# Seven products for the query weights and for the later convolution's second group, paired splits, and query norms moved into the sigmoids

## The chip, the cores and the metric

The kernel runs on one core of one Trainium2 chip. The core has a matrix engine (TensorE, PE in the profile, with its weight loads as PEld), a vector engine (VectorE, DVE), a scalar engine (ScalarE, ACT), GpSimd (POOL) and a sync engine (SyncE, SP). DMAs are issued from the queues of SP, ACT and POOL. The metric is the time of one execution on the device in microseconds (us); lower is better.

## What is computed

Two layers, each on the same 512 tokens of width 2048. A layer normalises its input, multiplies it by one wide input matrix, feeds three mixers, joins them and multiplies by an output matrix; the result is added to the input. In short:

```python
h = rmsnorm(x, norm_g); proj = h @ w_in            # 512 x 2048 @ 2048 x 7696
y_conv = B * (conv3(C * H) + bias) * silu(G)        # 512 channels, width 3, causal
q = rmsnorm(sb_q, qn_g); k = rmsnorm(sb_k, kn_g)    # 8 heads of 128, norm over a head
z = (q * 128**-0.5) @ k.T                           # strictly causal
later = reversed_cumsum(log_sigmoid(-z)) - log_sigmoid(-z)
y_sb = (exp(log_sigmoid(z) + later) @ v) * silu(g)
y_gla = rmsnorm(gated_linear_attention(...)) * silu(gl_g)
x = x + concat(y_conv, y_sb, y_gla) @ w_out         # 2048 x 2048
```

Inputs and outputs are float32. The kernel works in pairs of float16 parts (a high part and what is left), so that each product of two such operands is three matmuls: high by high, high by low, low by high.

## The kernel before

**Weights.** The input matrix and the output matrix are taken in groups of 256 columns. Each layer has, in this order: six groups of the linear attention; four of the first convolution half (h, c, g, b); for each of four pairs of heads (j = 0 to 3) values, gate, queries and keys (v, g, q, k); four of the second convolution half, which the code calls `conv h 1`, `conv c 1`, `conv g 1` and `conv b 1`; and eight groups of the output projection. `fetch` (line 346) loads a group of 2 MB into one of two staging buffers, two groups ahead, from POOL's queue. While PE works on one group, the next is prepared: `wmax` sums squares on ACT (L366), `wscale` sums over partitions on POOL (L380) and forms a power of two, and the parts are made: the high part on ACT and the low part on DVE. The squares are tied behind the first matmul of the running group and the preparation behind a later one (`hook`, line 466).

**Plain groups** (`project_cols`, `project_toks`, `project_by_token`) use the parts as they are: 96 matmuls of 512 moving columns, or 192 of 256, for 2048 rows. `whi` and `wlo` make the parts in two halves of 128x2048 (L435 on ACT, L442 on DVE).

**Seven-product groups** (`project_quick`, line 749) cut input, weights and result into two by two quarters and form the result from seven quarter products in place of eight (the scheme of Strassen and Winograd). The sums of the inputs are made once a layer (`xsums`, `msums`); they live in a buffer that the loaded mix of the branches takes later. The sums of the weights are made for each group in `wsums` (line 471): one addition by an accumulating DMA issued on POOL (L503) for the input matrix, the others on DVE (L506, L508, L511), and seven splits of 128x1024 (L485 on ACT, L486 on DVE). The names in `QUICK_IN` (line 31) and `QUICK` say which groups go this way: before, the gates and the keys of all pairs, `conv h 1`, and three and four groups of the output projection. The seven products go into four accumulators, pa and pd in one PSUM bank of 512 columns, pb and pf in another; between them ACT and DVE copy and add the intermediate results into the output tile (L778 to L792).

**Attention.** The queries and keys of a pair are projected (line 1298 on). For each, ACT squares every head of every token with a sum (L1318), DVE forms a reciprocal square root with three Newton steps on 8 columns (`rsqrt_bits`), and multiplies it into the tile: once for the queries (L1327), in eight products with the gains for the keys (L1332). Then high and low parts are made and SP transposes them by DMA (L1341). `attend` queues four later steps, which run after the following groups through `go`: `scores` for each of two heads, then `values` for each. `scores` takes the four query tiles of a head in two chunks of two tiles (`CHUNKS`): the products with the keys (L1226), the causal mask, two sigmoids (L1234, L1236), running products along the keys (L1239), a product, parts, and their transposes (L1247). `values` multiplies with v (L1263), then with the gate (L1270).

**The mix.** Each branch's result is scaled and split (`mixsplit`) and, until `mixload` (line 881), written to DRAM. `mixload` issues six loads on SP, after the group `conv h 1`. After the gate of the second convolution half, `weight_ratio` finds one common scale (L178) and rescales what was loaded, and the output projection follows.

**Order.** Outside of the first stretch, a planner in the compiler's front end puts each engine's instructions in order by its own estimate of their times; the order in the text gives the priority, and the preparation of weights is raised above it. On the chip every engine goes through its own queue in that fixed order, and waits at semaphores.

## Time and profile before

| what | value |
| --- | --- |
| median of 3 runs | 1718.91 us (1718.07 to 1722.91) |
| the profiled execution | 1717.69 us |
| its span, first to last instruction | 1715.9 us |
| mean granted clock of PE | 0.992 |
| DMA packets, bytes | 181478, 227.26 MB |
| chain: PE, DVE, DMA, ACT, issue | 73%, 12%, 7%, 4%, 3% |

A row of a group reads: line, engine, operation, output<-inputs, shapes, count, then busy us, the mean ns of one, and the engine's idle time before them with what ended it. A row of a window reads: the window in us from the span's start, its length, the busy time of PE, PEld, DVE, ACT and POOL with counts, the granted share of PE's clock, the mean busy share of the 16 DMA engines, and GB/s. A row of the timeline reads: start, length, engine, line, operation; in square brackets the engine's idle time before it and what ended it. Matmuls are pipelined, so a row's length is longer than the distance between the starts of two.

### The profile page before, as it was taken

Reading aid. Unit: us, or ns where it says so; the run is one execution under the profiler, and the core shown is the slowest. Engines: PE = TensorE matmul, PEld = TensorE weight load, DVE = VectorE, ACT = ScalarE, POOL = GpSimd, SP = SyncE. Lnnn points to the kernel's source line nnn. Section 1 sums busy time; section 2 is a strip of 40 time slices with the busy share of each in tenths; the row PEclk is TensorE's granted clock in tenths of the full one; section 3 lists DMA queues with packets and bytes.
Section 4 is the critical chain, followed back from the end, with each engine's and each line's share of the span. In section 5 each row is a group of like instructions: output and inputs, shape, how many; then the busy total and the mean of one; then the engine's idle time right before and its main releaser. Section 6 shows DMA issues by size and latency. Waiting matters only on the chain.

```text
span 1715.9 us, 36876 instructions
## 1 busy us (share of the span) xinstructions
PE 1669.9 (97%) x15642; PEld 1298.4 (76%) x15642; DVE 1331.3 (78%) x2327; ACT 1129.1 (66%) x1619; POOL 239.2 (14%) x286
## 2 busy tenths in 40 slices
PE   7999999999999989999989999999999999899999
PEld 5644548989898964799976455689898889548998
DVE  8975889877878767785688677997786888677883
ACT  7667677767666656666665676776765767565662
POOL 1211111111111111001122101121111111101110
PEclk9999999999999999999999999999999999999999
DMA  7233323566766686245543332446666667753441
GB/s 251 83 114 98 99 64 99 145 116 152 136 149 139 147 233 164 77 150 181 186 103 108 116 102 75 118 123 125 148 136 105 146 132 150 201 153 108 162 151 50
DMA packets 181478, 227.26 MB, mean 132 GB/s; under 512 B 94194, under 2 KB 141628, under 8 KB 180800
## 3 DMA queue, kind: packets, MB, share of 16 engines
q0 software_dynamic: 60352, 168.83, 34.4%
q1 hardware_dynamic: 111952, 46.61, 14.4%
q10 hardware_dynamic: 9008, 9.45, 1.7%
q8 instruction: 122, 2.00, 0.5%
q14 instruction: 44, 0.36, 0.1%
HBM read 179.65 MB, written 14.68 MB: 113 GB/s over the span
## 4 chain that ended last, share of the span: by engine, by line
PE 73%; DVE 12%; DMA 7%; ACT 4%; issue 3%; POOL 0%; DVEq 0%; ACTq 0%
PE psp L767 13%; PE psp L674 8%; PE psp L675 8%; PE psp L673 8%; PE psp L685 7%; PE psp L684 7%; PE psp L683 7%; PE psp L814 6%; PE psp L764 3%; DMA st<-in_w_in_dram 2%; DVE wl L486 2%; DMA th<-za 2%; DMA kT<-qp 2%; ACT junk L366 1%; DVE wl L442 1%
## 5 line engine op out<-in xcount | busy, mean ns | idle before, releaser
L366 ACT ACTIVATE junk<-st 128x2048 uint8<-128x2048 f32 x150 | 285.1, 1901 | 44.1 <-DMA st<-in_w_in_dram 42.8
L442 DVE SCALAR_TENSOR_TENSOR wl<-st,ws,wh 128x2048 f16<-128x2048 f32 x102 | 239.2, 2347 | 80.7 <-ACT wh L435 80.7
L435 ACT ACTIVATE wh<-st,ws 128x2048 f16<-128x2048 f32 x100 | 199.3, 1998 | 105.4 <-PE psp L674 47.1
L684 PE MATMUL psp<-wl,m 128*128 128x256 f16 x960 | 261.7, 273 | 0.0
L683 PE MATMUL psp<-wh,m 128*128 128x256 f16 x960 | 261.7, 273 | 0.0
L685 PE MATMUL psp<-wh,m 128*128 128x256 f16 x960 | 261.7, 273 | 0.0
L485 ACT ACTIVATE wh<-st,ws 128x1024 f16<-128x1024 f32 x150 | 167.6, 1143 | 120.5 <-DVE st L506 57.7
L486 DVE SCALAR_TENSOR_TENSOR wl<-st,ws,wh 128x1024 f16<-128x1024 f32 x150 | 189.6, 1279 | 27.4 <-ACT wh L485 27.3
L355 POOL DMA_DIRECT2D st<-in_w_in_dram x114 | 102.2, 900 | 436.0 <-DVE wl L442 319.4
L683 PE MATMUL psp<-wh,x 128*128 128x256 f16 x512 | 139.6, 273 | 0.0
L684 PE MATMUL psp<-wl,x 128*128 128x256 f16 x512 | 139.6, 273 | 0.0
L685 PE MATMUL psp<-wh,x 128*128 128x256 f16 x512 | 139.6, 273 | 0.0
L675 PE MATMUL psp<-x,wl 128*128 128x512 f16 x352 | 134.4, 382 | 2.2 <-DVE zun L186 2.2
L674 PE MATMUL psp<-x,wh 128*128 128x512 f16 x352 | 134.4, 382 | 0.0
L673 PE MATMUL psp<-x,wh 128*128 128x512 f16 x352 | 134.0, 381 | 0.0
L673 PE MATMUL psp<-m,wh 128*128 128x512 f16 x352 | 133.9, 380 | 0.0
L674 PE MATMUL psp<-m,wh 128*128 128x512 f16 x352 | 133.9, 380 | 0.0
L675 PE MATMUL psp<-m,wl 128*128 128x512 f16 x352 | 133.9, 380 | 0.0
L675 PEld LDWEIGHTS <-wl 128*128 128x128 f16 x704 | 69.2, 98 | 85.0 <-DVE wl L442 2.7
L673 PEld LDWEIGHTS <-wh 128*128 128x128 f16 x704 | 69.2, 98 | 81.5 <-issue 3.1
L380 POOL PARTITION_ALL_REDUCE wgm<-wm x75 | 40.0, 533 | 648.2 <-ACT junk L366 633.6
L674 PEld LDWEIGHTS <-wh 128*128 128x128 f16 x704 | 69.2, 98 | 80.8 <-issue 2.3
(427 smaller groups left out, 4042.2 us busy)
## 6 DMA issues: line engine op xcount, KB each, us to landing
st<-in_w_in_dram POOLq DMA_DIRECT2D x114, 1024.0 KB, 8.4
st<-in_w_out_dram POOLq DMA_DIRECT2D x32, 1024.0 KB, 7.4
st<-st POOLq DMA_DIRECT2D x18, 512.0 KB, 8.3
st<-in_w_in_dram SPq DMA_DIRECT2D x6, 1024.0 KB, 12.0
mixd<-g POOLq DMA_DIRECT2D x24, 256.0 KB, 7.7
x<-in_x_dram SPq DMA_DIRECT2D x4, 1024.0 KB, 4.9
qT<-in_x_dram ACTq DMA_DIRECT2D x8, 512.0 KB, 3.8
qT<-xs ACTq DMA_DIRECT2D x8, 512.0 KB, 3.9
```

What stands on the lines that cost most here:

```text
L366: sq = S.activation(junk(HK * GW).rearrange("p (k n) -> p k n", k=HK), staged[i][h], AF.Square, accum_out=peak[i][:, h:h + 1])
L435: hi = S.activation(wh[:, :, :GW], staged[i][h], AF.Copy, scale=scales[i])
L442: V.scalar_tensor_tensor(wl[:, :, :GW], staged[i][h], scales[i], wh[:, :, :GW], ALU.mult, ALU.subtract)
L485: hi = S.activation(h_, b, AF.Copy, scale=sc)
L486: V.scalar_tensor_tensor(l_, b, sc, h_, ALU.mult, ALU.subtract)
L673: T.matmul(o, wh[:, kk, cs], xh[:, :, k, :], start=st_, stop=False)
L674: T.matmul(o, wh[:, kk, cs], xl[:, :, k, :], start=False, stop=False)
L675: mm = T.matmul(o, wl[:, kk, cs], xh[:, :, k, :], start=False, stop=en)
L683: T.matmul(o, ah[:, t, k, :], wh[:, kk, :n], start=st_, stop=False, skip_group_check=True)
L684: T.matmul(o, ah[:, t, k, :], wl[:, kk, :n], start=False, stop=False, skip_group_check=True)
L685: return T.matmul(o, al[:, t, k, :], wh[:, kk, :n], start=False, stop=en, skip_group_check=True)
L767: mm = T.matmul(o[:, t * P:(t + 1) * P], a[p_][:, t, kk, :], w[q_][:, kk, :], start=st_, stop=en, skip_group_check=True)
```

## The change

- The queries of all four pairs and `conv c 1` become seven-product groups, in both layers: ten groups more.
- `fetch` lays such a group out with the quarters side by side, so that two quarters are adjacent; it takes three DMAs instead of two. `wsums` splits two quarters at once: three splits of 128x2048 and one of 128x1024 instead of seven of 128x1024. In the output projection the order of the additions is that of the input projection.
- The product into pf goes ahead of the first one into pb, and the preparation of the next group is tied behind it.
- The queries are no longer divided by their norms: the gains go onto the queries, the norms of the queries become the scale of the sigmoids, one column for each query tile and head, so each sigmoid is split by query tile. One reciprocal square root on 16 columns serves queries and keys, after the keys.
- The second chunk of a head takes its query tiles in falling order, so that `values` ends in one operation instead of two.
- `mixload` is called after `conv c 1` instead of after `conv h 1`.

```diff
-QUICK_IN = ("g 0", "k 0", "g 1", "k 1", "g 2", "k 2", "g 3", "k 3", "conv h 1")
+QUICK_IN = ("conv h 1", "conv c 1") + tuple(f"{n} {j}" for n in "gqk" for j in range(4))
-CHUNKS = ((((3, 0), (2, 512)), (3, 2)), (((0, 0), (1, 128)), (0, 1)))
+CHUNKS = ((((3, 0), (2, 512)), (3, 2)), (((1, 0), (0, 256)), (1, 0)))
...
+        if i in quick:
+            w = src[l, :, c0:c0 + GW].rearrange("(k r p) n -> p r k n", p=P, r=2)
+            own = whole[i].rearrange("p (k r) c -> p k (r c)", r=2)
+            for o, r, c in ((0, 1, slice(P, GW)), (P, 0, slice(0, GW)), (P + GW, 1, slice(0, P))):
+                queue.dma_start(own[:, :, o:o + c.stop - c.start], w[:, r, :, c])
+            st.extend(own[:, :, h * GW:(h + 1) * GW] for h in range(2))
+            return
...
-        G.dma_start(out=b12, in_=b11, accum_op=ALU.add)
-        split(b11, 0)
-        split(b22, 3)
+        if specs[i][1] is w_out:
+            V.tensor_tensor(b12, b12, b11, ALU.add)
+        else:
+            G.dma_start(out=b12, in_=b11, accum_op=ALU.add)
+        split(own[:, :, :2 * P])
         V.tensor_tensor(b22, b12, b22, ALU.add)
-        split(b22, 1)
         V.tensor_tensor(b11, b22, b11, ALU.subtract)
-        split(b11, 2)
-        split(b21, 4)
+        split(own[:, :, :2 * P])
+        split(own[:, :, 2 * P:])
         V.tensor_tensor(b21, b22, b21, ALU.add)
-        split(b12, 5)
-        split(b21, 6)
+        split(b21)
...
             prod(pa, w11, a11, True)
             S.activation(y12, za, AF.Copy)
-            hook(prod(pb, wT2, s_, True))
+            hook(prod(pf, w22, a12_s, True))
+            prod(pb, wT2, s_, False)
             V.tensor_tensor(y21, zb, y12, ALU.subtract)
             prod(pd, wT3, a11_21, False)
             S.activation(y22, zd, AF.Copy)
-            prod(pf, w22, a12_s, False)
             prod(pa, w21, a12, False)
             S.activation(y11, za, AF.Copy)
             prod(pb, wt1, a21_22, False, True)
...
-            if j:
-                mixload()
             then()
             uc = wk([P, 2, seq], "raw", 1) if j else wk([P, 2, seq], "zw")
             ps, u = project(True, lambda: uc)
...
+            if j:
+                mixload()
...
-                    S.activation(a, z[:, :zw], AF.Sigmoid, scale=nzun[:, l:l + 1])
                     w = wk([P, zw], "zw")
-                    S.activation(w, z[:, :zw], AF.Sigmoid, scale=zun[:, l:l + 1])
+                    for m, dst in ((0, a), (8, w)):
+                        for t, o in qtiles:
+                            ts_ = slice(o, o + (t + 1) * P)
+                            S.activation(dst[:, ts_], z[:, ts_], AF.Sigmoid,
+                                         scale=qz[:, m + 2 * t + hh:m + 2 * t + hh + 1])
...
-                rs = sm(8, "qr")
-                rsqrt_bits(rs, sq, u2, 8, "q")
-                V.tensor_scalar(rs, rs, u, None, ALU.mult)
-                if gain is None:
-                    r8 = raw.rearrange("p a (h c) -> p (a h) c", c=P)
-                    V.tensor_tensor(r8, r8, rs.rearrange("p (a o) -> p a o", o=1).to_broadcast([P, 8, P]), ALU.mult)
+                V.tensor_scalar(rm[:, 8 * n:8 * n + 8], sq[:, 8 * n:8 * n + 8], u2, EPS, ALU.mult, ALU.add)
+                r8 = raw.rearrange("p a (h c) -> p (a h) c", c=P)
+                if not n:
+                    qu = sm(1, "qu")
+                    V.tensor_scalar(qu, u, nzun[:, l:l + 1], 2.0 ** 25, ALU.mult, ALU.mult)
+                    by = kg[:, l, :].rearrange("p (o c) -> p o c", o=1)
                 else:
-                    for t in range(NT):
-                        for hh in range(2):
-                            rp = raw[:, t, hh * P:(hh + 1) * P]
-                            V.scalar_tensor_tensor(rp, rp, rs[:, 2 * t + hh:2 * t + hh + 1], gain, ALU.mult, ALU.mult)
...
+                    rs = rsqrt_bits(rm, "q")
+                    qz = sm(16, "qz")
+                    V.tensor_scalar(qz[:, :8], rs[:, :8], qu, None, ALU.mult)
+                    V.tensor_scalar(qz[:, 8:], qz[:, :8], -1.0, None, ALU.mult)
+                    V.tensor_scalar(rs[:, 8:], rs[:, 8:], u, None, ALU.mult)
+                    by = rs[:, 8:].rearrange("p (a o) -> p a o", o=1)
+                V.tensor_tensor(r8, r8, by.to_broadcast([P, 8, P]), ALU.mult)
```

More of the change, by code (lines that the diff above doesn't have):

```diff
@@ L473, in wsums @@
         sc = scales[i]
[L474 removed]
+        own = whole[i].rearrange("p (k r) c -> p k (r c)", r=2)
+        b22, b11, b12, b21 = (own[:, :, n * P:(n + 1) * P] for n in range(4))
         parts = loaded[i][0]
[L476 to L478 removed]
@@ L503, in wsums, with split @@
-        G.dma_start(out=b12, in_=b11, accum_op=ALU.add)
-        split(b11, 0)
-        split(b22, 3)
+        def split(src):
+            n = src.shape[2] // P
+            if n == 1:
+                pair = [wk([P, HK * P], t, 1, dt=F16) for t in ("w7h", "w7l")]
+            else:
+                pair = [wpool.tile([P, HK, GX], F16, tag=t, name=nm(t)).rearrange("p k c -> p (k c)")[:, :HK * n * P]
+                        for t in ("wh", "wl")]
+            h_, l_ = (a.rearrange("p (k c) -> p k c", c=n * P) for a in pair)
+            S.activation(h_, src, AF.Copy, scale=sc)
+            V.scalar_tensor_tensor(l_, src, sc, h_, ALU.mult, ALU.subtract)
+            parts.extend([a[:, :, m * P:(m + 1) * P] for a in (h_, l_)] for m in range(n))
@@ L1297, in hybrid_trunk @@
             qkT = []
-            for gain in (None, kg[:, l, :]):
+            sq, rm = sm(16, "qs"), sm(16, "qrm")
+            for n in range(2):
                 raw = []
                 def dst():
-                    raw.append(wk([P, NT, GW], *(("raw", 1) if gain is None else ("kT",))))
+                    raw.append(wk([P, NT, GW], *(("kT",) if n else ("raw", 1))))
                     return raw[0]
@@ L1343, in hybrid_trunk @@
                 go()
-            attend(j, *qkT, vh, vl, vu, g, s_)
+            attend(j, *qkT, qz, vh, vl, vu, g, s_)
         conv_out(1, conv_in(1, go), go)
```

56 lines of the change are left out of this document (15 added, 41 removed).

## The prediction

> **What bounds the kernel now.** I read the busy table and the chain of waits first, to see which engine sets the end; then single weight groups, to price one group on TensorE (PE); then PE's waits; then the vector engine (DVE) and the scalar engine (ACT) over one pair of heads, to see what room they have.
>
> ```profile
> span 1715.9 us, 36876 instructions
> PE 1669.9 (97%) x15642; PEld 1298.4 (76%) x15642; DVE 1331.3 (78%) x2327; ACT 1129.1 (66%) x1619; POOL 239.2 (14%) x286
> PE 73%; DVE 12%; DMA 7%; ACT 4%; issue 3%; POOL 0%; DVEq 0%; ACTq 0%
> ```
>
> PE is busy 97% of the span and holds 73% of the chain: work taken off PE counts, as long as the others keep up. Windows cut at the first matmul of a group and of the next one:
>
> ```profile
> core 0: us, PE busy (x) PEld busy (x) DVE busy (x) ACT busy (x) POOL busy (x), PEclk, DMA share, GB/s
> 327.56:346.32 18.76, 18.76 (x338) 18.75 (x336) 15.94 (x31) 15.91 (x31) 4.33 (x5) 1.00 0.50 133
> 346.32:367.28 20.96, 20.96 (x195) 18.80 (x193) 14.11 (x33) 10.98 (x18) 2.00 (x2) 1.00 0.92 159
> 657.38:678.10 20.72, 20.72 (x99) 9.41 (x97) 15.86 (x25) 11.16 (x14) 2.30 (x3) 1.00 0.55 114
> 433.00:519.00 86.00, 85.73 (x951) 77.87 (x949) 69.20 (x125) 59.71 (x94) 14.29 (x17) 1.00 0.67 145
> ```
>
> The first row is the keys of pair 0, a group by seven products (336 matmuls, the count takes in neighbours at the edges; PE never idle): 18.76 us. The second is a plain group by tokens, values of pair 1 (192 matmuls): 20.96 us, 0.1092 us each. The third is a plain group by columns, gate of the later convolution (96 matmuls, 20.72 us). The last is one whole pair of heads (keys to keys): PE 85.73 of 86.00, DVE 69.20, ACT 59.71.
>
> **The PE term.** Eight query groups go from 20.96 to 18.76: 8 x 2.20 = 17.6 us. The later convolution's second group becomes 7 x 24 = 168 matmuls of 256 columns instead of 96 of 512: 168 x 0.1092 = 18.3 against 20.7, so 2 x 2.4 = 4.8 us. Together **-22.4 us**. Everything else must be hidden beside PE, or it comes off this.
>
> **The load of the mix halves, moved behind one more group.**
>
> ```profile
> PE psz L1226 <- DMA kT<-qp: 11.0, 2, 5.9
> 530.73 3.93 SPq L1341 DMA_TRANSPOSE kT<-qp  x2
> 617.17 7.09 SPq L887 DMA_DIRECT2D m<-mixd  x4
> 625.02 13.34 SPq L1341 DMA_TRANSPOSE kT<-qp  x2
> 640.15 0.69 PE L1226 MATMUL psz<-kT,qT 128*128 128x512 f16 x2 [5.87 <-DMA kT<-qp]
> 634.00:641.00 7.00, 1.13 (x5) 0.36 (x3) 0.63 (x1) 0.00 (x0) 0.00 (x0) 0.82 1.22 190
> 641.00:656.00 15.00, 15.00 (x65) 6.60 (x64) 8.94 (x12) 7.01 (x7) 1.78 (x2) 0.86 0.61 206
> 1493.00:1507.00 14.00, 14.00 (x65) 6.39 (x64) 8.34 (x11) 6.42 (x7) 1.79 (x2) 0.92 0.65 216
> ```
>
> PE's two longest waits inside the layers (11.0 us, one per layer) are the last pair's first scores waiting for the key transposes. In pair 2 SP handles the two key transposes in 3.93 us; in pair 3 four loads of the mix stand ahead, the DMA share is 1.22, and they take 13.34. After each wait the granted clock is low: 0.86 over 15 us and 0.92 over 14 us, so 0.14 x 15 + 0.08 x 14 = 3.2 us more. The six loads now come after the second convolution group (they must: that group reads the input sums whose buffer they overwrite), so nothing stands ahead of these transposes. With 4 us instead of 13 they land some 9 us earlier, and the 5.9 us wait goes: **-14.3 us** (11.0 + 3.2). Bounds: all of it, or nothing, if the DVE chain ahead of the transposes is now later by as much. What is late next: the loads meet the score transposes, and the rescaling of the mix needs them.
>
> ```profile
> 684.48 0.37 POOL L178 PARTITION_ALL_REDUCE rgm<-pmix  x1 [6.65 <-DVE pmix L186]
> m<-mixd SPq DMA_DIRECT2D x4, 512.0 KB, 15.8
> ```
>
> The rescaling starts at 684.5; the loads can start when the second convolution group ends, near 640, and 15.8 us to landing leaves some 25 us. I cost this at nothing; without that cover each layer would wait for the rest.
>
> **What the vector and scalar engines get instead** (one pair of heads, grouped by shape):
>
> ```profile
> L486 DVE SCALAR_TENSOR_TENSOR wl<-st,ws,wh 128x1024 f16<-128x1024 f32 x12 | 15.1, 1280 | 1.5 <-ACT wh L485 1.5
> L442 DVE SCALAR_TENSOR_TENSOR wl<-st,ws,wh 128x2048 f16<-128x2048 f32 x4 | 9.4, 2348 | 0.0
> L506 DVE TENSOR_TENSOR st<-st 128x1024 f32<-128x1024 f32 x2 | 2.5, 1225 | 0.4 <-DMA st<-st 0.3
> L1332 DVE SCALAR_TENSOR_TENSOR kT<-kT,qr,kg 128x128 f32<-128x128 f32 x8 | 2.2, 347 | 0.0
> L1327 DVE TENSOR_TENSOR raw<-raw,qr 128x1024 f32<-128x1024 f32 x1 | 1.2, 1226 | 0.0
> L216 DVE TENSOR_TENSOR qrt<-qr 128x8 f32<-128x8 f32 x6 | 1.0, 166 | 0.2
> L792 DVE TENSOR_TENSOR kT<-psp,kT 128x256 f32<-128x256 f32 x1 | 0.4, 423 | 0.0
> L485 ACT ACTIVATE wh<-st,ws 128x1024 f16<-128x1024 f32 x12 | 13.4, 1144 | 11.9 <-DVE st L506 8.4 <-DVE ws L396 1.7 <-PE psp L685 1.6
> L435 ACT ACTIVATE wh<-st,ws 128x2048 f16<-128x2048 f32 x4 | 8.0, 2004 | 2.2 <-PE psp L767 1.3 <-PE psp L764 0.9
> L1236 ACT ACTIVATE zw<-psz,zun 128x896 f32<-128x896 f32 x2 | 2.0, 998 | 0.0
> L1236 ACT ACTIVATE zw<-psz,zun 128x384 f32<-128x384 f32 x2 | 1.2, 588 | 0.0
> ```
>
> DVE: preparing a seven-product group costs 7 x 1.28 + 3 x 1.22 = 12.6 us now, and in pairs 3 x 2.35 + 1.28 + 3 x 1.22 = 12.0; a plain one 2 x 2.35 = 4.7. A pair of heads goes from two of each (34.6) to three and one (40.7): +6.0. The queries' assembly adds five operations of 0.42 (+2.1); one Newton chain of nine steps of 0.166 goes (-1.5; its few scalings about cancel against the new scale columns); the keys' eight products (2.2) become one like the queries' (1.2): -1.0; merging the value outputs saves 0.2. Net +5.4: 74.6 of the 83.8 us that PE would then need, 89%. ACT: preparation 2 x 7 x 1.14 + 4 x 2.0 = 24.0 becomes 3 x (3 x 2.0 + 1.14) + 4.0 = 25.4; the sigmoids split by query tile, eight more starts, each at the part that doesn't scale (0.998 - 896 x 0.41/512 = 0.28): +2.2. So 59.7 + 3.6 = 63.3 of 83.8. POOL gets one more accumulating transfer per pair and a third issue per fetch, of 14.3 busy in 86. In its queue a fetch waits for the last split of the group whose buffer it takes:
>
> ```profile
> 467.74 1.80 POOL L355 DMA_DIRECT2D st<-in_w_in_dram  x2 [7.62 <-DVE w7l L486]
> ```
>
> Behind it stand the next group's sum over partitions and accumulation. With three such groups running, one late DVE split (here 12 us into the gate, 455.7) moves the next group's; the product order, which now needs the weight sums 5.3 instead of 2.6 us into a group, gives back what the shorter query group takes (2.2). The queries' transposes, without the norm ahead of them, only start earlier. All this lies beside PE as long as DVE's own waits shrink from 16.8 us per pair (86.0 - 69.2) to 9.2. If they don't, that is a rival below.
>
> **The new order of the products.** A group has two PSUM banks: one holds the accumulators pa and pd, the other pb and pf.
>
> ```profile
> PE psp L764 <- ACT g L785: 5.5, 6, 1.9
> 508.23 0.22 PE L767 MATMUL psp<-wl,s 128*128 128x128 f16 x1
> 509.53 0.37 ACT L782 ACTIVATE kT<-psp 128x256 f32<-128x256 f32 x1
> 468.36 0.38 PE L764 MATMUL psp<-s,wh 128*128 128x256 f16 x2
> 468.58 0.27 PE L764 MATMUL psp<-x,wh 128*128 128x256 f16 x1
> ```
>
> The last product writes pd, and waits 5.5 us in 6 groups for ACT's read of pa (L785), the other half of the bank, although a product of 2.6 us in the other bank lies between: writes wait for reads of the whole bank. Before, every change from one accumulator of a bank to the other had such a product between. Now pf goes ahead of pb, and after the third weight sum's product into pd comes ACT's copy of pd (L782), and straight after it a product into pa. In the keys of pair 2 that copy ends at 509.90, 1.6 us after the product's last matmuls (508.2): ACT was in a 2.0 us split. Bounds over 35 groups (28 of the input, 7 of the output projection): 35 x 1.6 = 56 us, if PE takes the products in the order of the text; at best nothing, and today's waits of this kind (5.5) go too. For a value: PE's instructions are not in the order of the text. In the gate of pair 2 (the last two rows) matmuls on the sums (s) of a later product run up to the start of the product on x: the planner fills such gaps with what is ready, and PE lost nothing there. The product into pb, 2.6 us, can fill here. I take 0.5 us a group, nearer the filled end: 17.5 less today's 5.5, **+12 us**.
>
> [...]
>
> **Sum:** -22.4 - 14.3 + 12 = -24.7. The profiled execution took 1717.7 (span 1715.9, 1.8 around it), so 1693; the median of the runs shown, 1718.9, is 1.2 above it: **1694 us**.
>
> **Rivals.**
> - The full gain: fillers cover every bank change as in the gate above and today's 5.5 us stay: 1718.9 - 36.7 = 1682, down to 1677 if they go as well. For it: PE lost nothing in the keys' window. Against: each group now has two such changes and one filler.
> - The key wait stays: the second convolution group's preparation (7.3 us more on DVE) delays the keys' chain, and the scores wait as now: 1694 + 14.3 = 1708. For it: DVE is busy 23.4 of 29 us there, by the row below. Against: 9 us of transposes go.
>
> ```profile
> 605.00:634.00 29.00, 28.36 (x224) 21.08 (x221) 23.36 (x49) 22.32 (x34) 5.22 (x7) 1.00 0.75 215
> ```
>
> - Slower: PE waits out ACT's copy of pd in each of 35 groups, unfilled. It decides from (36.7 + 5.5) / 35 = 1.2 us a group on; at 1.6 us, less today's 5.5, it costs 50: 1718.9 - 36.7 + 50 = 1732. For it: the order in the text, and ACT's splits grow from 1.14 to 2.0 us. Against: the filled gap at 468.4.
> - DVE becomes the bound: its waits stay at 16.8 us, a pair takes 74.6 + 16.8 = 91.4 instead of 83.8, and eight pairs lose 61 in place of the 12: 1718.9 - 36.7 + 61 = 1743. For it: the first of these preparations still waits for an accumulating transfer of 8.3 us to land, now in three groups running. Against: in a seven-product group of the output projection between two others (second row), DVE is busy 16.67 of 18.74, the same 89%, and PE loses nothing.
>
> ```profile
> st<-st POOLq DMA_DIRECT2D x18, 512.0 KB, 8.3
> 1653.83:1672.57 18.74, 18.74 (x337) 18.63 (x334) 16.67 (x23) 12.37 (x15) 2.19 (x3) 1.00 0.53 171
> ```
>
> **How the numbers follow.** Forecast 0.46 (1685 to 1702), full gain 0.15, key wait 0.20 (up to 1712), unfilled banks 0.13, DVE 0.06. A measurement of this kernel tells about 0.3% (5 us) from no change. Faster: the first three, 0.81; within 0.3% 0.05, the lighter part of the unfilled case (1714 to 1724); slower 0.14, the rest of it and DVE. The range leaves out half of the full gain and the far part of the slower cases: 1677 to 1724.
>
> **What would show it.** Right: query groups of 18.8 us without PE idle; no wait of scores for key transposes in either layer, and no low clock behind it; DVE near 75 us a pair of heads, ACT near 63. Wrong: PE waits for ACT's copy of pd in most groups (banks), waits for the low parts of weights from DVE (DVE bound), or waits for the mix after the later convolution; or the 11 us stand at the same scores.

## The result, and the profile after

The changed kernel takes 1770.19 us (median of 4 runs, 1761.78 to 1772.53) against 1718.49 (4 runs): a ratio of 1.0292, 95% interval 1.0249 to 1.0334. It is 51.7 us slower where 25 us of gain were forecast. From its page, span, busy times and the chain by engine:

```profile
span 1768.6 us, 39523 instructions
PE 1668.4 (94%) x16938; PEld 1326.9 (75%) x16938; DVE 1378.2 (78%) x2216; ACT 1153.8 (65%) x1642; POOL 292.3 (17%) x331
PE 20%; DMA 10%; DVE 9%; ACT 6%; issue 5%; POOL 1%; SPq 0%; ACTq 0%; DVEq 0%; POOLq 0%
```

PE's share of the chain fell from 73% to 20%. PE's idle time is span less busy: 46.0 before (1715.9 - 1669.9), 100.2 after, so +54.2. The mean granted clock went from 0.992 to 0.983; span x (1 - clock) is 13.7 before and 30.1 after. Part of this low clock falls into PE's idle time. Counted by the trace's clock records only while PE is busy, it took 11.2 us before and 25.8 after, so +14.6. Busy time fell by 1.5 although the clock took 14.6, so the products became cheaper by 16.1. These make the 52.7 us of span: -16.1 + 14.6 + 54.2. The count is good to some 5 us: the six kernels below with the same products as before come to 1659 to 1663 us of work by it, before to 1658.6.

One pair of heads (keys of pair 1 to keys of pair 2), then inside it the queries' group of pair 2 with the scores around it, and the keys behind it:

```profile
418.62:514.40 95.78, 87.09 (x1096) 80.86 (x1094) 73.70 (x113) 63.09 (x99) 18.33 (x20) 0.96 0.65 138
490.58:514.40 23.82, 19.26 (x326) 18.64 (x324) 21.18 (x28) 18.45 (x31) 4.19 (x4) 1.00 0.60 95
514.40:539.15 24.75, 22.58 (x360) 22.22 (x358) 17.98 (x25) 17.28 (x26) 3.92 (x5) 0.93 0.63 158
```

DVE works 73.70 us and ACT 63.09 per pair; 74.6 and 63.3 were worked out. But the pair takes 95.78 us instead of 83.8, and DVE's waits grew from 16.8 to 22.1. PE's waits in the whole run, by what ended them:

```profile
engine line waited for: us in total, times, longest us
PE psp L762 <- ACT raw L773: 13.7, 6, 2.3
PE psp L762 <- DVE wl L495: 12.7, 14, 2.2
PE psp L759 <- ACT qT L773: 10.4, 2, 5.7
PE psp L762 <- ACT wh L494: 10.1, 8, 2.0
PE psp L809 <- DMA m<-raw: 5.5, 2, 4.8
PE psz L1221 <- DMA kT<-qp: 5.0, 4, 2.2
```

The wait for the key transposes fell from 11.0 to 5.0. New are waits for copies out of PSUM (L773) and for the parts of weights (L494 on ACT, L495 on DVE). What holds ACT up is in the row of its squares:

```profile
L373 ACT ACTIVATE junk<-st 128x2048 uint8<-128x2048 f32 x150 | 285.5, 1904 | 97.4 <-DMA st<-in_w_in_dram 90.3
```

Before and after, they wait for a fetch (us in total, times, longest):

```profile
ACT junk L366 <- DMA st<-in_w_in_dram: 42.8, 17, 5.6
ACT junk L373 <- DMA st<-in_w_in_dram: 90.3, 34, 6.0
```

How such a wait reaches PE, in the timelines of POOL, DVE, ACT and PE around the queries of pair 2:

```profile
478.41 1.28 DVE L495 SCALAR_TENSOR_TENSOR w7l<-st,ws,w7h 128x1024 f16<-128x1024 f32 x1
479.99 2.69 POOL L357 DMA_DIRECT2D st<-in_w_in_dram  x3 [5.98 <-DVE qu L1320]
```

```profile
490.08 1.91 ACT L373 ACTIVATE junk<-st 128x2048 uint8<-128x2048 f32 x1 [3.32 <-DMA st<-in_w_in_dram]
...
492.50 1.16 ACT L1233 ACTIVATE za<-psz,qz 128x512 f32<-128x512 f32 x2 [0.42 <-DMA th<-za]
493.55 3.89 ACT L494 ACTIVATE wh<-st,ws 128x2048 f16<-128x2048 f32 x2
498.37 1.92 ACT L373 ACTIVATE junk<-st 128x2048 uint8<-128x2048 f32 x1
...
502.70 0.41 ACT L773 ACTIVATE raw<-psp 128x256 f32<-128x256 f32 x1
```

```profile
503.17 0.22 PE L762 MATMUL psp<-wh,s 128*128 128x128 f16 x1 [2.28 <-ACT raw L773]
```

The gate group's last split, 9.6 us after that group began on PE (468.82), ends at 479.7 and frees a staging buffer. (The fetch's row names `qu`, a 0.2 us instruction two places behind the split in DVE's order; of the two it is the split that reads the buffer.) The fetch of the keys' weights starts, and ACT's squares of them stand idle for 3.32 us until what they read has landed at 490. Nothing of those squares is needed by PE in this group. But behind them in ACT's order come sigmoids, high parts and, at 502.70, the copy that frees PE's bank. From 490.08 to 502.70 ACT hardly stops (0.42 us idle), so it cannot win the 3.32 us back, and PE loses 2.28 of them.

A wait of these squares is not new. In the kernel before they stand 3.76 us at the same group, with a copy for PE close behind:

```profile
473.78 1.91 ACT L366 ACTIVATE junk<-st 128x2048 uint8<-128x2048 f32 x1 [3.76 <-DMA st<-in_w_in_dram]
...
475.69 0.36 ACT L785 ACTIVATE g<-psp 128x256 f32<-128x256 f32 x1
```

There PE had 24 products of the plain queries' group to do meanwhile (473.06 to 476.11) and waited 0.3 us. Nor does this fetch come later: it started 12.0 us into its gate before (467.74), and 11.2 here. Two other things are new. The next fetch, of the values of pair 3, takes the buffer of the queries. As a plain group these had their last low part ready, and the buffer free, 5 us ahead of the main run of their products (478.72); as a seven-product group they free it 18.7 us after their first product (490.58). Before and after:

```profile
473.74 1.76 POOL L355 DMA_DIRECT2D st<-in_w_in_dram  x2 [4.19 <-DVE wl L442]
```

```profile
509.31 1.78 POOL L362 DMA_DIRECT2D st<-in_w_in_dram  x2 [6.35 <-DVE w7l L495]
```

And in a fetch laid out by quarters the first squares read parts of two of the three transfers. These had landed 8.8 us after the first issue (median of 28 fetches); before, the first of two transfers was enough, after 6.9 us (median of 57).

PE stood still from 500.89 (503.17 - 2.28), and the copy it waited for started at 502.70, behind `zw` (from 500.87, 0.75 us) and `ga` (from 501.47, 1.36 us) on ACT.

### The profile page after: what moved, and what is told of

Its sections match the earlier page's. It is cut to its first block, busy times and chain, and to the rows that moved or that the text cites. A ratio compares the mean times of both kernels' runs of the same rounds, so it can differ in the third digit from the quotient of the medians.

```text
span 1768.6 us, 39523 instructions
## 1 busy us (share of the span) xinstructions
PE 1668.4 (94%) x16938; PEld 1326.9 (75%) x16938; DVE 1378.2 (78%) x2216; ACT 1153.8 (65%) x1642; POOL 292.3 (17%) x331
## 4 chain that ended last, share of the span: by engine, by line
PE 20%; DMA 10%; DVE 9%; ACT 6%; issue 5%; POOL 1%; SPq 0%; ACTq 0%; DVEq 0%; POOLq 0%
DMA st<-in_w_in_dram 4%; PE psp L809 3%; PE psp L668 3%; PE psp L669 3%; PE psp L670 3%; DMA th<-za 3%; ACT junk L373 2%; DVE wl L495 2%; ACT wh L494 2%; PE psp L762 2%; PE psp L759 1%; PE psp L680 1%; PE psp L678 1%; PE psp L679 1%; DMA st<-in_w_out_dram 1%
## 5 line engine op out<-in xcount | busy, mean ns | idle before, releaser
L373 ACT ACTIVATE junk<-st 128x2048 uint8<-128x2048 f32 x150 | 285.5, 1904 | 97.4 <-DMA st<-in_w_in_dram 90.3
L495 DVE SCALAR_TENSOR_TENSOR wl<-st,ws,wh 128x2048 f16<-128x2048 f32 x105 | 245.2, 2349 | 60.3 <-ACT wh L494 60.1
L449 DVE SCALAR_TENSOR_TENSOR wl<-st,ws,wh 128x2048 f16<-128x2048 f32 x82 | 192.0, 2347 | 71.1 <-ACT wh L442 71.0
L494 ACT ACTIVATE wh<-st,ws 128x2048 f16<-128x2048 f32 x105 | 207.3, 1995 | 61.2 <-DVE st L504 45.8
L762 PE MATMUL psp<-wh,s 128*128 128x128 f16 x2048 | 190.7, 225 | 26.8 <-ACT raw L773 13.7
L762 PEld LDWEIGHTS <-s 128*128 128x128 f16 x3072 | 185.1, 101 | 34.5 <-issue 34.3
L442 ACT ACTIVATE wh<-st,ws 128x2048 f16<-128x2048 f32 x80 | 158.1, 1994 | 75.6 <-DVE ws L403 28.3
L679 PE MATMUL psp<-wl,m 128*128 128x256 f16 x704 | 192.6, 274 | 3.1 <-DVE wl L449 3.1
L762 PE MATMUL psp<-wl,s 128*128 128x128 f16 x1024 | 184.2, 225 | 11.3 <-DVE wl L495 11.3
L680 PE MATMUL psp<-wh,m 128*128 128x256 f16 x704 | 192.6, 274 | 0.0
L678 PE MATMUL psp<-wh,m 128*128 128x256 f16 x704 | 192.6, 274 | 0.0
L759 PE MATMUL psp<-s,wh 128*128 128x256 f16 x768 | 137.9, 281 | 12.0 <-ACT qT L773 10.4
L762 PEld LDWEIGHTS <-m 128*128 128x128 f16 x2160 | 123.1, 98 | 5.5 <-issue 5.1
L669 PE MATMUL psp<-x,wh 128*128 128x512 f16 x320 | 121.3, 379 | 0.0
L668 PE MATMUL psp<-x,wh 128*128 128x512 f16 x320 | 121.1, 379 | 0.0
```

The costliest lines, as they stand in the source:

```text
L373: sq = S.activation(junk(HK * GW).rearrange("p (k n) -> p k n", k=HK), staged[i][h], AF.Square, accum_out=peak[i][:, h:h + 1])
L449: V.scalar_tensor_tensor(wl[:, :, :GW], staged[i][h], scales[i], wh[:, :, :GW], ALU.mult, ALU.subtract)
L494: S.activation(h_, src, AF.Copy, scale=sc)
L495: V.scalar_tensor_tensor(l_, src, sc, h_, ALU.mult, ALU.subtract)
L668: T.matmul(o, wh[:, kk, cs], xh[:, :, k, :], start=st_, stop=False)
L669: T.matmul(o, wh[:, kk, cs], xl[:, :, k, :], start=False, stop=False)
```

## The experiments

Eighteen kernels, in the order in which they were run. For the table each wait of PE over 0.25 us after the first 100 us was followed back through the order of the engine that ended it: idle stretches there are added, nearest first, until they make up the wait, and each is booked to the transfer that ended it. "Squares" are waits that go back so to squares waiting for a fetch, "sigmoids" to sigmoids waiting for the score transposes, "scores" are waits of the scores for the key transposes. The expectations from e_th on quote an older way of following, which booked a whole wait to the first idle stretch it met, however short; for the kernel after it gave 35.2 and 26.4 where the finer way gives 47.9 and 10.8. This matters below. Each ratio is to runs of before taken beside that kernel. The columns behind it are from one profiled execution; that of b_norm (1729.2) took 11 us less than the median, that of b_ordcq (1740.4) 8 less, those of e_sq (1799.7) and b_ordcqge (1724.7) 7 and 5 more.

| run | median us | ratio to before (95%) | PE idle | span x (1 - clock) | squares | sigmoids | scores |
| --- | --- | --- | --- | --- | --- | --- | --- |
| before | 1718.9 | | 46.0 | 13.7 | 5.8 | 4.2 | 11.0 |
| after | 1770.2 | 1.0292 (1.0249 to 1.0334) | 100.2 | 30.1 | 47.9 | 10.8 | 5.0 |
| e_noq | 1788.8 | 1.0393 (1.0349 to 1.0438) | 98.8 | 30.3 | 20.2 | 21.1 | 15.0 |
| e_sq | 1793.0 | 1.0418 (1.0368 to 1.0467) | 123.8 | 39.6 | 23.4 | 18.3 | 14.8 |
| e_sx | 1778.5 | 1.0331 (1.0288 to 1.0374) | 103.4 | 35.6 | 15.6 | 20.4 | 22.5 |
| e_dve | 1808.9 | 1.0542 (1.0469 to 1.0614) | 126.2 | 43.2 | 53.3 | 11.0 | 1.4 |
| b_ord | 1713.8 | 0.9981 (0.9960 to 1.0003) | 39.8 | 8.5 | 5.1 | 0 | 3.2 |
| b_pair | 1748.5 | 1.0181 (1.0154 to 1.0207) | 62.4 | 22.7 | 4.7 | 25.0 | 9.0 |
| b_norm | 1740.4 | 1.0128 (1.0084 to 1.0172) | 55.2 | 22.5 | 4.4 | 3.7 | 22.5 |
| b_q | 1729.0 | 1.0065 (1.0040 to 1.0090) | 66.6 | 22.4 | 2.4 | 0.5 | 13.7 |
| e_th | 1741.5 | 1.0147 (1.0113 to 1.0182) | 79.6 | 17.4 | 22.7 | 15.0 | 4.3 |
| e_sxth | 1751.8 | 1.0209 (1.0179 to 1.0239) | 83.2 | 26.3 | 10.8 | 11.6 | 17.9 |
| b_ordmix | 1716.7 | 1.0004 (0.9985 to 1.0022) | 43.4 | 6.8 | 5.0 | 2.6 | 4.3 |
| b_ordc | 1706.5 | 0.9946 (0.9928 to 0.9965) | 41.8 | 6.8 | 11.9 | 1.7 | 1.2 |
| b_th | 1708.7 | 0.9958 (0.9936 to 0.9979) | 36.8 | 11.9 | 0 | 0 | 13.9 |
| bp_th | 1713.9 | 0.9979 (0.9955 to 1.0003) | 41.1 | 13.7 | 4.2 | 0 | 8.6 |
| e_nopair | 1742.9 | 1.0147 (1.0109 to 1.0184) | 76.0 | 31.4 | 35.8 | 10.0 | 4.0 |
| b_ordcq | 1748.3 | 1.0180 (1.0125 to 1.0235) | 77.8 | 29.6 | 25.7 | 25.9 | 0 |
| f_ge | 1761.5 | 1.0246 (1.0204 to 1.0288) | 92.3 | 26.4 | 42.2 | 0 | 5.7 |
| b_ordcqge | 1719.5 | 1.0009 (0.9985 to 1.0033) | 66.5 | 19.0 | 9.7 | 0 | 2.9 |

### Four edits of the kernel after

**e_noq**: the queries plain again.

```diff
-QUICK_IN = ("conv h 1", "conv c 1") + tuple(f"{n} {j}" for n in "gqk" for j in range(4))
+QUICK_IN = ("conv h 1", "conv c 1") + tuple(f"{n} {j}" for n in "gk" for j in range(4))
```

> The queries go back to plain groups; all else of the change stays (paired splits, product order, norms, second convolution group by seven products). Queue theory and chain theory both: with no third seven-product group in a row in the heads, most of the 50 us of PE waits there go, and with them the low clock; PE gets 8 x 2.2 = 17.6 us more to do: 1725 to 1740. If the heads' waits come from the product order or the paired splits instead, they stay in gates and keys: 1765 or more.

1788.8, another 18.6 slower: idle time stays (98.8), and the products' gain is lost. Other waits came: scores 15.0, sigmoids 21.1. The queries' third group in a row is not what makes the change slow by itself.

**e_sq**: the squares of the next weights ordered on ACT behind the second split of this group.

```diff
+                if i - 1 in split23:
+                    order(a, split23[i - 1])
```

> Only the order of ACT's queue is changed: the squares of the next group's weights stand behind the split of the second pair of quarters (the weight sums of the second and third product) of the running group. Queue theory (ACT's fixed order puts a square that waits for its fetch ahead of that split, so the split and the bank copies behind it are late): PE's waits for the high and low parts, 29 us, fall below 10, those for the first bank copy, 26 us, fall too: 1720 to 1745. Chain theory (fetch, squares, sum, accumulation, additions, splits take longer than one seven-product group whatever the order): the next preparation only starts later, 1765 to 1785.

1793.0. Squares fell from 47.9 to 23.4 and 18.5 us of direct waits of PE for score transposes came, with 14.8 at the scores. With one waiting instruction moved, others came up in other places.

**e_sx**: the squares of a part of the groups read the projections' input instead of the fetched weights (scaled by a constant), so the scales of those weights are not from their own squares. The expectation names g 0 to conv b 1. But the edit counts 34 groups a layer where there are 38: it takes g 0 to k 3 in the first layer, and the second group of the first convolution half to k 2 in the second.

```diff
+        if i % 34 in range(11, 26) and cur:
+            src_, f_ = cur[0][:, h, :, :], 1.67e-4
+            sq = S.activation(junk(HK * GW)..., src_, AF.Square, scale=f_, accum_out=peak[i][:, h:h + 1])
```

> From the gate of pair 0 to the fourth group of the second convolution half, the squares of the next weights read as many elements of the transposed input instead of the fetched weights (so the scale of these weights is not that of their own squares). ACT's work is the same, but no square waits for a fetch. Queue theory: ACT's idle time before squares (90 us) falls by half or more, PE's waits for parts and bank copies (55 us) fall below 15: 1715 to 1735. Chain theory with the accumulation and DVE as its long parts: the fetch still comes first, 1750 or more.

1778.5. The squares' waits fell to 15.6, and nothing was won: scores 22.5 (5.0 after), sigmoids 20.4. ACT's own waits at squares for fetched input weights fell from 90.3 to 54.1 us only, by the groups that the edit leaves out, so the fall by half or more that the queue theory starts from did not come, and the run does not decide it.

**e_dve**: the first weight sum on DVE everywhere, not by an accumulating DMA.

```diff
-        if specs[i][1] is w_out:
-            V.tensor_tensor(b12, b12, b11, ALU.add)
-        else:
-            G.dma_start(out=b12, in_=b11, accum_op=ALU.add)
+        V.tensor_tensor(b12, b12, b11, ALU.add)
```

> The first sum of the weights of the input groups is made on DVE (1.2 us) instead of by the accumulating transfer (about 7 us to landing), as the output groups already do. Chain theory: each preparation is 6 us shorter, PE's waits for parts (29 us) mostly go: 1725 to 1745. Queue theory: the additions end earlier, but the split still stands behind the waiting square: 1760 to 1772. DVE as the bound: 28 x 1.2 = 34 us more for DVE, 1780 or more.

1808.9, the slowest of all, with the transfer of 6.9 us taken away. Squares still wait (53.3), and PE now waits 29.5 us for the score transposes directly. Taking the transfer away is no cure; but DVE has 28 additions more, some 34 us, so the run does not price the transfer by itself. In the kernel after, 1.1 us of PE's waits go back to it.

### One part at a time on the kernel before

**b_ord**: the order of the products alone. **b_pair**: the paired quarters, the layout of the fetch in three pieces and the additions' order. **b_norm**: the norms as the sigmoids' scale, one Newton chain, and the second chunk's order. **b_q**: the queries by seven products, with single quarters.

```diff
-            hook(prod(pb, wT2, s_, True))
+            hook(prod(pf, w22, a12_s, True))
+            prod(pb, wT2, s_, False)
```

> The kernel before with the new product order alone (the product into pf ahead of the first into pb). Order theory (with two changes inside a bank left to one filler, PE waits for ACT's bank copies; 37 us of such waits after against 6 before): these waits rise by 10 us or more, 1732 or more. If the order is harmless: 1714 to 1726.

> The kernel before with the paired quarters alone (fetch in three pieces, three splits of 128x2048 and one of 128x1024), old product order. Pair theory (the high and low parts of the second and third product come only after both additions and a split of twice the length, and ACT is held 2.0 us at a time): PE's waits for parts and bank copies rise by 10 us or more, 1732 or more. If pairing is harmless: 1712 to 1724, since DVE saves 0.6 us in each of 25 groups.

> The kernel before with the query norms as the sigmoids' scale, one Newton chain, and the second chunk's order alone. Harmless by every theory so far: 1712 to 1724; a sigmoid theory (twice as many starts hold up ACT's queue) would give 1730 or more.

> The kernel before with the four query groups by seven products alone, by the old fetch, splits and order. If the product term stands once the rest is left out: 1700 to 1708. If three such groups in a row can't be prepared in time (chain theory): 1725 or more, with PE waits for parts at queries and keys.

The order costs nothing: 0.9981 (0.9960 to 1.0003). The others lose 31.8, 23.6 and 12.2 us against the runs of before beside them (1716.8), each by another wait. The norms: 22.5 us at the last pair's scores, twice the 11.0. The queries: PE's work falls by 16.3 (busy time less the low clock in it: 1658.6 before, 1642.3), and idle time takes more than that back, 20.6, most of it in waits for copies out of PSUM (16.8 in the largest row). The pairs have the plainest profile, PE's waits first:

```profile
PE psp L759 <- ACT g L780: 25.0, 6, 9.5
PE psz L1221 <- DMA kT<-qp: 9.0, 2, 5.1
```

and the timelines of SP, ACT and PE at one of those six places, the gate of pair 1:

```profile
383.57 8.85 SPq L1242 DMA_TRANSPOSE th<-za  x4
```

```profile
400.59 1.01 ACT L1229 ACTIVATE za<-psz,nzun 128x896 f32<-128x896 f32 x1 [12.16 <-DMA th<-za]
401.50 1.00 ACT L1231 ACTIVATE zw<-psz,zun 128x896 f32<-128x896 f32 x1
402.39 0.38 ACT L780 ACTIVATE g<-psp 128x256 f32<-128x256 f32 x1
```

```profile
402.82 0.37 PE L759 MATMUL psp<-x,w7h 128*128 128x256 f16 x1 [9.47 <-ACT g L780]
```

The second head's sigmoid writes tile `za`, of which there are two; the 16-bit parts of the first head's weights lie in the same tiles, and their transposes are still running; the third of the four lands at 400.49. ACT stands 12.16 us at that write with PE's copy two instructions behind it, and PE stands 9.47.

### Taking the sigmoids' wait away, and its control

**e_th**, **b_th** and **bp_th**: after, before and the pairs alone, with the high parts transposed only; the products with the values take the high part twice. **e_sxth**: e_th with the edit of e_sx.

```diff
-                    for i, part in enumerate((wh, wl)):
+                    for i, part in enumerate((wh,)):
...
-                        for i, (a_, b_) in enumerate(((vh, 0), (vh, 1), (vl, 0))):
+                        for i, (a_, b_) in enumerate(((vh, 0), (vh, 0), (vl, 0))):
```

> The kernel after with half of the score transposes: the low parts of the weights of the attention are computed and not transposed, and the products with the values take the high part twice, so TensorE has as many products as before. Theory (ACT's first sigmoids of a second head stand in front of the bank copies and wait until the four transposes of the first head have read the tile): TensorE's waits that go back to a sigmoid waiting for a score transpose, 26.4 us after, fall below 8, and with the low clock behind them the time falls by 25 to 35, to about 1740. Rival 1 (another wait takes their place: with ACT earlier, the squares wait longer for their fetch): their sum falls but that of the squares, 35.2, grows by as much, and the time stays within 10 us of 1770. Rival 2 (the sigmoids' waits are short beside ACT's own amount of work): the 26.4 stand.

> The same, and the squares from g 0 to conv b 1 read the projections' input in place of the fetched weights, so that they don't wait for a fetch (the scales of those weights are then not from their own squares). Theory (instructions on ACT that wait for a landing transfer, ahead of bank copies and splits, make TensorE's 97 us of idle time): with both kinds gone, waits with these two roots fall from 61.6 to below 20, idle time to 45 to 65 and the time to 1715 to 1735. Rival (the amount of work on ACT and DVE is the limit, and the landing transfers only name it): idle time stays above 85 with other roots, among them bank copies and splits behind additions, and the time stays above 1755.

> A control: the kernel before with half of the score transposes (the low parts of the weights of the attention are computed and not transposed; the products with the values take the high part twice). Theory (the sigmoids' waits for the score transposes came with the change; before they cost 4.2 us of TensorE's idle time): 1708 to 1718. Rival (half of the transposes makes any version of this kernel faster, by the load that it takes from the queues): 1685 to 1695, 25 less or more, and the 28.7 that the same edit brought after says nothing of the change.

> The kernel before with the paired quarters alone (1748.54) and with half of the score transposes as in the control. Theory (its 25.0 us of waits that go back to sigmoids waiting for score transposes, with the low clock behind them, are what the pairs lose): these waits below 8, 1715 to 1730. Rival (they are moved to other roots): 1740 to 1755.

The control gains 7.0 us on before (ratio 0.9958); the pairs gain 34.7 (1748.5 to 1713.9), their 25.0 us of waits go, and of the 31.8 that they cost 5.2 are left (1713.9 - 1708.7). The edit hardly changes the order on the engines here: of ACT's 1226 instructions 1204 stand in the same order in b_pair and bp_th, of DVE's 2252 2186. For the pairs alone the sigmoids' wait is the cause.

e_th gained 28.7, the size expected, but not in the way expected: its sigmoids still cost PE 15.0 us, and it was the squares' waits that fell, from 47.9 to 22.7. ACT's own waits in e_th:

```profile
ACT junk L373 <- DMA st<-in_w_in_dram: 61.8, 24, 5.6
...
ACT za L1233 <- DMA th<-za: 28.2, 9, 4.5
```

The time came true and the reason did not. In e_sxth, whose squares are those of e_sx, 22.4 us are left of these two (squares 10.8, sigmoids 11.6; the kernel after has 58.7), and the time fell to 1751.8 only, worse than e_th: 17.9 us had come up at the scores.

### The parts together, and a cure

**b_ordmix**: the order and the later place of the mix's load. **b_ordc**: the order and the later convolution's second group by seven products, with the mix's load behind it. **b_ordcq**: that and the queries. **e_nopair**: the whole change without the pairs.

```diff
-QUICK_IN = ("g 0", "k 0", "g 1", "k 1", "g 2", "k 2", "g 3", "k 3", "conv h 1")
+QUICK_IN = ("g 0", "k 0", "g 1", "k 1", "g 2", "k 2", "g 3", "k 3", "conv h 1", "conv c 1")
...
-            if j:
-                mixload()
             then()
...
+            if j:
+                mixload()
             y = wk([P, 2, seq], "kT")
```

> The kernel before with two parts of the change: the order of products (the second product of a group last of the first bank) and the load of the mix moved ahead of the second group of the later convolution, which stays plain. Theory (the load of the mix delays the keys' transposes in the second layer, 11.0 us before and 3.2 with the order alone): waits of scores for key transposes below 3, the low clock behind them gone, 1700 to 1710. Rival (the planner moves the wait, as in the runs so far): 1712 to 1722.

> The kernel before with three parts of the change: the order of products, the second group of the later convolution by seven products, and the mix loaded ahead of it; no queries, no pairs, no norms. Theory (those two parts do what the prediction said, 4.5 us of products and the key wait; the loss comes with pairs, norms and queries): 1698 to 1708. Rival (one more group that is prepared costs its waits on ACT wherever it stands): 1714 to 1730.

> The kernel before with the order of products, the later convolution's second group and the queries by seven products; no pairs, no norms. Theory (the queries' 17.9 us of products are lost again in ACT's and DVE's waits for the transfers of the preparation, as alone, where they came to +11): 1712 to 1725. Rival (with the order the queries pay, as they do in the kernel after, where undoing them cost 18.6): 1686 to 1697.

> The kernel after with the paired quarters and the three-piece fetch undone: four parts of the change (order, later convolution, queries, norms) stay. Theory (the pairs' longer instructions and the later places of transposes behind them lose 25 to 35 in each company, as alone): 1735 to 1748. Rival (the norms and queries lose as much without the pairs, since every part only moves waits): 1755 to 1775.

In the program of b_ordmix and b_ordc the load of the mix comes one group later than before, as the diff shows; "ahead of" in the two expectations is a slip. On the chip b_ordmix is b_ord again: the planner leaves the loads where they were, ahead of the key transposes, and all five engines have the same instructions in the same order. So it says nothing of the load, and it shows what two runs of one order differ by: ratios 0.9981 and 1.0004, scores 3.2 and 4.3, sigmoids 0 and 2.6. In b_ordc the loads do stand behind. SP in b_ordmix, then in b_ordc:

```profile
619.48 15.15 SPq L887 DMA_DIRECT2D m<-mixd  x6
634.74 9.20 SPq L1341 DMA_TRANSPOSE kT<-qp  x2
```

```profile
634.98 4.27 SPq L1341 DMA_TRANSPOSE kT<-qp  x2
640.50 17.23 SPq L887 DMA_DIRECT2D m<-mixd  x6
```

b_ordc is faster than both kernels: 1706.5, ratio 0.9946 (0.9928 to 0.9965). Its waits at the scores are 1.2 us, and PE is busy 98% of the span:

```profile
PE 1663.0 (98%) x15786; PEld 1311.6 (77%) x15786; DVE 1345.6 (79%) x2353; ACT 1136.6 (67%) x1635; POOL 250.8 (15%) x288
```

The queries on top of it cost 41.8 us (median against median; both ranges of the expectation were missed), with 25.9 of idle time by the sigmoids and 25.7 by the squares, though they save PE's work. Without the pairs the whole change takes 27.3 less (1770.2 to 1742.9): the pairs lose about the same in company as alone.

**f_ge** and **b_ordcqge**: after, and b_ordcq, with the two 16-bit parts in tiles of their own. All transposes stay; a sigmoid then waits for DVE only, and the copy into `ga`, later in ACT's order, for the transposes.

```diff
-                    parts = a.bitcast(F16)
...
-                    wh, wl = parts[:, :zw], parts[:, 896:896 + zw]
+                    wh, wl = (wk([P, 896], tag, dt=F16)[:, :zw] for tag in ("ga", "e"))
```

> The whole change, complete, with the two 16-bit parts of the attention's weights in tiles of their own (tags ga and e) in place of the sigmoids' tile za: a sigmoid then waits for DVE alone, and what waits for the score transposes of two chunks before is ACT's copy into ga, some us later in ACT's order. All transposes stay. Theory (the place of the wait in ACT's order costs, not the transposes' time): TensorE's waits that go back to L1233 waiting for th<-za, 26.4 us, below 5, those that go back to the copy below 10, and 1735 to 1750. Rival 1 (the copies hold up ACT as the sigmoids did): 1760 to 1775. Rival 2 (ga and e are also needed by the sigmoids of the gates and the values' results, whose waits take their place): 1755 to 1780, with new roots there.

> The same edit on the kernel with the order of products, the later convolution's second group and the queries by seven products (1748.3; 29.5 us of idle time go back to the sigmoids), complete and correct in what it computes. Theory: the 29.5 below 8, 1708 to 1722, since the squares' 22.2 us of waits stay. Rival (the waits move to the copies or to other roots): 1735 to 1750.

In b_ordcq it is worth 28.8 us (1748.3 to 1719.5). The planner made a new order with it (1291 of ACT's 1365 and 2195 of DVE's 2457 instructions stand in the same order), so not all of this is the tile's. Squares fall too, from 25.7 to 9.7, and PE now waits 22.9 for the score transposes itself, at the values:

```profile
PE psm L1262 <- DMA th<-e: 22.9, 6, 7.6
PE psp L814 <- DMA m<-raw: 6.7, 1, 6.7
```

In the kernel after it is worth 8.7, with intervals that overlap. No sigmoid of the scores waits for transposes on ACT any more, the copies wait 19.1 us, and the squares' 90.3 us stay:

```profile
ACT junk L373 <- DMA st<-in_w_in_dram: 88.9, 31, 9.7
...
ACT ga L1241 <- DMA th<-ga: 19.1, 2, 10.0
```

The time is that of its rival 1, but PE loses only 4.9 us by the copies: what stays is the squares' wait for the fetch, 42.2.

## Why the prediction was wrong

- **The PE term held roughly in size.** -22.4 was forecast; PE's work fell by 16.1 in the whole change and by 16.3 in b_q (17.6 for the queries there), by a count that is good to some 5 us. The later convolution with the mix's load behind it won 6 us on the order alone (ratios 0.9981 and 0.9946), or 10 against the order's second run (1.0004).
- **The key wait held in part.** -14.3 was forecast as 11.0 of wait and 3.2 of clock behind it. The wait fell to 5.0 after and 1.2 in b_ordc. The clock gained nothing in the whole change: low clock took 25.8 us of PE's busy time after and 11.2 before, with new waits beside it. The forecast took the load of the mix for the cause, and half of it holds: the key transposes take 4.27 us with the loads behind them (b_ordc), 9.2 with the loads ahead (b_ord, b_ordmix). But most of the wait, 11.0 to 3.2 and 4.3, went with the order of the products alone, the loads still ahead.
- **The banks.** The +12 for the new order of products was put down to copies that PE could not fill. Waits for copies did come, 24.1 us in the two largest rows (L773). But b_ord shows that the order alone costs nothing, so the +12 and the slower rival as they were told, unfilled banks from the order, are wrong there; in the whole change the order was not undone by itself. Followed back, most of PE's waits come from ACT standing at a transfer.
- **The step that failed** is "All this lies beside PE as long as DVE's own waits shrink from 16.8 us per pair (86.0 - 69.2) to 9.2." The work was right to 1 us a pair on DVE and 0.2 on ACT, but DVE's waits grew to 22.1, and 74.6 + 9.2 became 95.8. So the waits of the added preparation, put at nothing, are the term that failed; "a fetch waits for the last split of the group whose buffer it takes" was seen, with three such groups running, and not priced. The rival with DVE as the bound came nearest, at 1743 with a chance of 0.06; it had DVE's waits stay at 16.8 and looked at DVE, and what waits is mostly ACT (58.7 of PE's 83.0 us go back to squares and sigmoids). Sums of busy time cannot show this: ACT is busy 63 of 96 us, and its waits for transfers stand in the order ahead of the copies and splits that PE needs next.
- **What the runs put in its place.** For the pairs alone it is shown that they lose by sigmoids standing on score transposes (bp_th against b_th), and for order, convolution and queries that an edit which moves this wait to a later instruction, and with it the planner's order, gives 28.8 of 41.8 us back (b_ordcqge). The norms alone lose with 22.5 us at the scores; their trace has the last pair's second key transpose behind loads of the mix, 13.01 us long, but what delays it was not tried by itself. In the whole change the largest traced wait is the squares' for the fetch, 47.9 of 83.0 us. The trace shows what is late: the queries' buffer comes free 18.7 us into their group instead of ahead of it, and in a fetch by quarters the data of the first squares lands after 8.8 us instead of 6.9, while one transfer takes what it took before (8.0 us to landing, 8.4 before). That this is the cause of the whole loss is not shown, and stays open: e_sx made only a part of the squares independent of the fetch, e_dve paid for a shorter turn with more work on DVE, and both were slower, with other waits in place. A third staging buffer or a third `za` would test it; neither was tried, nor the layout of the fetch apart from the splits (b_pair, with the same layout, has squares at 4.7).
- **Parts do not add.** The queries cost 12.2 alone and 41.8 beside b_ordc, and win 18.6 in the whole change. All but one of the edits (b_ordmix) make a new order, and the order decides which transfer stands in front of PE's next copy.

## What to carry to other kernels

Before paying for less work on the bound engine with more work on engines that have room, list the instructions of these engines that wait for a transfer, and what stands behind each in its queue: one that feeds the bound engine can make the transfer's lateness the bound engine's (in b_pair ACT stood 12.16 us and PE 9.47). Tiles that a transfer still reads should not be written by an instruction ahead of such work; parts in a tile of their own gave 28.8 us in one version here, and 8.7, within the spread, in another. Ask of each staging buffer when its last reader comes, before and after the change. Where a planner sets the order, try each part of a change alone and beside the others, and keep those that pay: here two of five did, together.

## What was not expected of the hardware

A stretch of low clock can come with a wait of PE of only about 2 us. Windows around one in the kernel after (PE's wait of 2.17 us ends at 522.27; the windows start at 516.0, 520.5 and 524.0):

```profile
516.00:520.50 4.50, 4.09 (x72) 3.90 (x70) 1.06 (x2) 4.50 (x4) 0.00 (x0) 1.00 0.88 202
520.50:524.00 3.50, 1.73 (x24) 1.73 (x24) 3.50 (x2) 3.50 (x10) 0.00 (x0) 0.87 0.00 0
524.00:527.40 3.40, 3.40 (x42) 3.40 (x41) 3.40 (x5) 2.74 (x5) 0.40 (x1) 0.64 0.02 5
```

```profile
522.27 0.22 PE L762 MATMUL psp<-wl,s 128*128 128x128 f16 x1 [2.17 <-DVE wl L495]
```

The low clock is 0.5 for 3.41 us here, from 523.06 (0.13 x 3.50 + 0.36 x 3.40 = 1.7 us lost, half of 3.4). Of the 16 waits of 2.0 to 2.4 us after the first 50 us of this kernel, 10 have such a stretch beside them; three of these 10 have another wait of about 2 us less than 6 us ahead. Of the eight waits between 1.5 and 2.0 one has it (2.4 us ahead of one of the 10), and of the four between 1.0 and 1.5 none. So 2.17 us of wait came with 1.7 us of low clock here, nearly 4 together. In the kernel before, after the first 100 us, the four waits of 3.55 to 5.87 us have such a stretch beside them and the five of 1.06 to 1.86 us none, and the forecast had counted low clock only behind the two of 5.87 and 5.16 us at the scores.
